# A small load of 64 KiB issued ahead of the first 8 MiB load of a row normalisation

## The chip, the cores and the metric

The kernel runs on one core of a Trainium2 chip. The metric is device time in microseconds (us), the median of several executions; lower is better.

## The reference

```python
x: 1024 x 4096 float32, eps = 1e-12
norm = sqrt(sum(x ** 2, axis=-1, keepdims=True) + eps)
out = (x / norm).astype(float32)
```

16 MiB are read and 16 MiB are written, with little arithmetic for each byte.

## The kernel before

The 1024 rows are cut into two tiles. Each of the 128 partitions of a tile holds four whole rows, which lie side by side in memory, so a load of a tile consists of 128 contiguous pieces of 64 KiB. Both tiles fit into SBUF, so both loads are issued at once:

```python
R = 4
n_tiles = N // (P * R)                                   # 2
x_t = x.rearrange("(p t r) d -> t p (r d)", t=n_tiles, r=R)
...
for i in range(n_tiles):
    g = RowGroups(nc, io, stats, scratch, D, R, eps_t)
    load = nc.sync.dma_start(out=g.flat(), in_=x_t[i])   # 128 pieces of 64 KiB
    to_front(nc, load.ins)
    groups.append(g)
```

`to_front` moves a load to the very front of SyncE's program, ahead of the barrier at which the engines of the core meet. For each tile VectorE squares and sums one row and ScalarE three; a square root and a reciprocal follow, and the rows are scaled in place. The last row of the first tile is scaled by both engines (ScalarE 7/8 of it). Then the tile is stored by one DMA:

```python
for i, g in enumerate(groups):
    g.square_dve(R - 1)
    g.square_act(0)
    g.norm(0)
    g.scale(0)
    ...                                                  # rows 1, 3 and 2 alike
    if i < n_tiles - 1:
        g.scale_by_both(2)                               # cut = 7 * D // 8
    else:
        g.scale(2)
    store = nc.sync.dma_start(out=out_t[i], in_=g.flat())
```

## Time and profile before

| | kernel before |
|---|---|
| time, median of 6 | 81.88 us (81.67 to 81.95) |
| span of the profiled execution | 79.9 us |
| share of the span in which the 16 DMA engines moved packets | 97.6% |
| VectorE, ScalarE busy | 33%, 37% |
| 32 rows of 16 packets of 64 KiB at 2.42 us | 77.4 us |

I call 16 packets, one on each DMA engine, a row (of packets; the rows of the matrix are another thing); the kernel has 32 of them, 8 for each load and each store. The compute engines mostly wait, and what they wait for is data. Here are the page's busy line, its memory line, and the two longest waits (engine and line, what it waited for, us in total, times, longest):

```profile
DVE 26.7 (33%) x21; ACT 29.7 (37%) x23; POOL 0.2 (0%) x4
HBM read 16.78 MB, written 16.78 MB: 420 GB/s over the span
```

```profile
DVE sq_dve L42 <- DMA xt<-in_x_dram: 25.7, 2, 20.4
ACT sq_act L33 <- DMA xt<-in_x_dram: 21.7, 2, 19.3
```

### The profile page before, as it was taken

The numbers are of one execution on the slowest core, as the hardware profiler recorded it, in microseconds if no ns is written. First come the engines' busy times: TensorE is split into PE (matmuls) and PEld (weight loads), VectorE is DVE, ScalarE is ACT, GpSimd is POOL, SyncE is SP. The second block draws the span as 40 slices with busy tenths as digits, with TensorE's granted clock in tenths as the row PEclk, the third lists the DMA queues.
The fourth block names the chain that finished last, engine by engine and source line by source line (L and its number), as shares of the span: only waits on it lengthen the run. The fifth ranks groups of instructions, "written<-read, shape, count | busy, mean of one in ns | idle before, by whom it ended". The sixth has DMA issues, their size and how long they took to land.

```text
span 79.9 us, 93 instructions
## 1 busy us (share of the span) xinstructions
DVE 26.7 (33%) x21; ACT 29.7 (37%) x23; POOL 0.2 (0%) x4
## 2 busy tenths in 40 slices
DVE  0000000000099599960049995999200000000000
ACT  3200000000099999989349999950000000000000
POOL 1000000000000000000000000000000000000000
DMA  9099996599996699993899991999974999965990
GB/s 492 33 525 525 525 525 295 230 525 525 525 525 262 262 525 525 525 525 164 361 525 525 525 459 66 525 525 525 525 328 197 525 525 525 525 295 230 525 525 0
DMA packets 576, 33.55 MB, mean 420 GB/s; under 512 B 64, under 2 KB 64, under 8 KB 64
## 3 DMA queue, kind: packets, MB, share of 16 engines
q1 hardware_dynamic: 576, 33.55, 97.6%
HBM read 16.78 MB, written 16.78 MB: 420 GB/s over the span
## 4 chain that ended last, share of the span: by engine, by line
DMA 51%; ACT 10%; DVE 9%; SPq 0%; issue 0%
DMA xt<-in_x_dram 51%; ACT sq_act L33 9%; DVE xt L64 9%; ACT rstd L53 1%; SPq L219 0%; DVE rstd L59 0%
## 5 line engine op out<-in xcount | busy, mean ns | idle before, releaser
L33 ACT ACTIVATE sq_act<-xt 128x4096 f32<-128x4096 f32 x6 | 21.7, 3609 | 21.7 <-DMA xt<-in_x_dram 21.7
L42 DVE SCALAR_TENSOR_TENSOR sq_dve<-xt 128x4096 f32<-128x4096 f32 x2 | 8.8, 4424 | 25.7 <-DMA xt<-in_x_dram 25.7
L64 DVE TENSOR_SCALAR xt<-xt,rstd 128x4096 f32<-128x4096 f32 x7 | 16.5, 2353 | 0.2
L72 ACT ACTIVATE xt<-xt,rstd 128x3584 f32<-128x3584 f32 x1 | 3.3, 3282 | 0.2 <-DVE rstd L59 0.2
L53 ACT ACTIVATE rstd<-ssq,eps_t 128x1 f32<-128x1 f32 x8 | 2.1, 289 | 0.1
L59 DVE RECIPROCAL rstd<-rstd 128x1 f32<-128x1 f32 x8 | 1.3, 159 | 2.4 <-ACT rstd L53 2.4
L33 ACT ACT_TABLE_LOAD x1 | 1.3, 1283 | 1.3 <-PEq L257 1.3
L53 ACT ACT_TABLE_LOAD x1 | 1.3, 1283 | 0.0
L33 ACT ACTIVATION_READ_ACCUMULATOR sq_act<-xt 128x1 f32 x6 | 1.1, 186 | 0.0
L211 DVE MEMSET eps_t<- 128x1 f32 x1 | 0.1, 59 | 1.3 <-PEq L257 1.3
L78 DVE TENSOR_SCALAR xt<-xt,rstd 128x512 f32<-128x512 f32 x1 | 0.5, 486 | 0.0
L42 DVE DVE_READ_ACCUMULATOR sq_dve<-xt 128x1 f32 x2 | 0.2, 82 | 0.0
L257 POOL MEMSET const-bfloat16-1.0<- 128x1 bf16 x1 | 0.1, 103 | 0.0
L257 POOL MEMSET const-uint8-127<- 128x1 uint8 x1 | 0.1, 102 | 0.0
L257 POOL MEMSET const-float32-0.0<- 128x1 f32 x1 | 0.1, 100 | 0.2 <-issue 0.2
L257 POOL MEMSET const-float32-1.0<- 128x1 f32 x1 | 0.1, 99 | 0.0
## 6 DMA issues: line engine op xcount, KB each, us to landing
xt<-in_x_dram SPq DMA_DIRECT2D x2, 31.2
out_dram<-xt SPq DMA_DIRECT2D x2, 22.5
```

The costliest lines, as they stand in the source:

```text
L33: self.nc.scalar.activation(out=sq_a, in_=self.x[:, r], func=ACT_F.Square, accum_out=self.ssq[:, r : r + 1],)
L42: self.nc.vector.scalar_tensor_tensor(out=sq_v, in0=self.x[:, r], scalar=1.0, in1=self.x[:, r], op0=ALU.mult, op1=ALU.mult, accum_out=self ...
L53: self.nc.scalar.activation(out=self.rstd[:, r : r + n], in_=self.ssq[:, r : r + n], func=ACT_F.Sqrt, bias=self.eps_t,)
L59: self.nc.vector.reciprocal(out=self.rstd[:, r : r + n], in_=self.rstd[:, r : r + n])
L64: self.nc.vector.tensor_scalar_mul(out=self.x[:, r], in0=self.x[:, r], scalar1=self.rstd[:, r : r + 1])
L72: self.nc.scalar.activation(out=self.x[:, r, :cut], in_=self.x[:, r, :cut], func=ACT_F.Copy, scale=rstd,)
L78: self.nc.vector.tensor_scalar_mul(out=self.x[:, r, cut:], in0=self.x[:, r, cut:], scalar1=rstd)
L211: nc.vector.memset(eps_t, eps)
L257: nc = _bacc.Bacc("TRN2", target_bir_lowering=False, num_devices=1)
```

## The change

The first 512 bytes of each of the 128 pieces of the first tile are loaded once more, into a tile that nobody reads, ahead of everything else. The intent: let a small load meet the slow start, so that the big one runs at full rate from its first byte.

```diff
+    heads = scratch_pool.tile([P, D // 32], F32)
+    to_front(nc, nc.sync.dma_start(out=heads, in_=x_t[0][:, : D // 32]).ins)
 
     groups = []
     for i in range(n_tiles):
```

## The prediction

> **What bounds the kernel now.** I read the page's queue part first, then the chain that ended last in order of time, then the two load issues, then short windows at the two ends of the span.
>
> The DMA queue (packets, MB, share of the span that 16 DMA engines were occupied) and the chain (start us, us, what):
>
> ```profile
> q1 hardware_dynamic: 576, 33.55, 97.6%
> ```
>
> ```profile
> 0.00 0.38 SPq L219
> 0.38 0.05 issue
> 0.43 40.69 DMA xt<-in_x_dram
> ```
>
> The queue has 16 engines occupied for 97.6% of 79.9 us, which is 78.0 us of the span. VectorE has 26.7 us and ScalarE 29.7 us of work, a third each. The chain continues from the second load through the arithmetic of the second tile and breaks off at the last scale, before the last store; but the stream of data is not interrupted while that arithmetic runs, because the first store is already queued at 38.71 us:
>
> ```profile
> 38.71 18.13 SPq L239 DMA_DIRECT2D out_dram<-xt  x2
> ```
>
> The two stores are issued at 38.71 and about 56.5 us (38.71 + 18.13 less one issue of 0.35). The first is issued before the second load has landed (41.1 us), the second before the first store is through (the 16 engines finish it at about 60 us). So compute is hidden, and the time is head + stream + tail of the DMA engines.
>
> Short windows show the head and the tail. The columns are the window, its length, the busy time of three engines, the clock, the DMA share and GB/s. From the values I infer that a packet is counted whole in the window in which it starts (a share of 4.34 can't be otherwise), so a window of 0.5 us gives both a count (GB/s times 0.5 us over 65,536 bytes) and a mean duration (share times 0.5 us times 16, over the count):
>
> ```profile
> 0.50:1.00 0.50, 0.00 (x0) 0.00 (x0) 0.00 (x0) 1.00 0.00 0
> 1.00:1.50 0.50, 0.06 (x1) 0.23 (x1) 0.00 (x0) 1.00 4.34 1442
> 1.50:2.00 0.50, 0.00 (x0) 0.50 (x1) 0.00 (x0) 1.00 1.29 524
> 2.00:2.50 0.50, 0.00 (x0) 0.50 (x1) 0.00 (x0) 1.00 0.30 131
> ...
> 4.00:4.50 0.50, 0.00 (x0) 0.00 (x0) 0.00 (x0) 1.00 4.23 1835
> 4.50:5.00 0.50, 0.00 (x0) 0.00 (x0) 0.00 (x0) 1.00 0.60 262
> ...
> 76.50:77.00 0.50, 0.00 (x0) 0.00 (x0) 0.00 (x0) 1.00 4.84 2097
> ```
>
> What to see: nothing starts before 1.00 us. Then 11 packets start by 1.50 (1442 x 0.5 / 65.5 = 11), 4 by 2.00 and one after 2.00: one for each of 16 engines, spread over more than half a microsecond. The 11 early ones last 4.34 x 0.5 x 16 / 11 = 3.16 us each, the 4 next 2.58, the last 2.4. The second row (14 + 2 packets from 4.00 on) lasts 4.23 x 8 / 14 = 2.42 us each, and so does the last row, whose 16 packets all start between 76.50 and 77.00. 32 rows of 2.42 are 77.4 us, the floor of this kernel. What is above it in the span: 1.0 us before the first packet, (4.34 + 1.29 + 0.30) x 8 / 16 = 2.97 us for the mean first packet against 2.42, so 0.55 us lost in the first row, some 0.4 us of spread between engines, and about half a microsecond after the last packet. The 1.9 us between span and measured time (79.9 against 81.77 in the profiled run) lie outside the program's instructions.
>
> A detail decides much below: early starters are slow, late starters are not. An engine that starts after 2.00 runs at full speed at once. So the first row's loss does not look like a fixed fee that each engine pays for its first packet; it looks like a phase, ending some 1.7 to 2.1 us after the first issue, before which no engine runs at full rate.
>
> **What the Trainium skill says.** "DMA: Bandwidth & Descriptors", section "Latency and other measured facts", gives about 600 ns to the first byte of a DMA issued from SyncE. The trace agrees: the first issue ends at 0.38 us and the first packets start just after 1.00, 0.62 later. The same page, "Where 436 GB/s comes from", puts the ceiling of the 16 engines at 435 GB/s; 16 x 65,536 bytes in 2.42 us are 433 GB/s, so the stream is at that ceiling and no change at its front can speed it up. The same page, "Queues, rings and completion order", says that each engine consumes descriptors in ring order: the head pieces come before the first big pieces on every engine. And its "Rules for kernel authors" warn that transfers under 64 KB are mostly overhead; the new load is 128 x 512 bytes, exactly 64 KiB. No run here shows yet what that costs on this path. I found no page that speaks of a slow first transfer or of warming one up.
>
> **The change, part by part.** It adds one load of 64 KiB in 128 pieces into a tile that nobody reads, and moves it to the very front, before the first big load. It removes nothing. The intent must be that the small load meets the slow phase, so that the big one runs at full speed from its first byte.
>
> Issue: a load's issue holds the SyncE queue for 0.38 to 0.43 us:
>
> ```profile
> L219 SPq DMA_DIRECT2D xt<-in_x_dram x2: 383/404/426, 0.0 to 0.4; - x2
> ```
>
> So the first big load is issued at about 0.43 us in place of 0.00, and its first packets can start at 1.00 + 0.43 = 1.43 at the earliest. Data: 4 KiB for each engine; at the measured 65,536 bytes in 2.42 us that is 0.15 us, an estimate without any fee per piece. It falls between 1.0 and 1.43, in which the engines would have nothing else, so on the path it costs little or nothing. The end: one more completion to be waited for, 16 small packets that land 78 us before the end; nothing. Compute: ScalarE and VectorE leave the start barrier about 0.4 us later (its table load starts at 1.26 and is over at 2.54), while the first data land at 21.8; nothing. Space: 512 bytes of a partition; nothing.
>
> What remains is the time at which each engine's first big packet ends. Now the mean first packet ends at about 1.3 + 2.97 = 4.27 (1.3 is my estimate of the mean start from the counts: 11 near 1.1, 4 near 1.7, one near 2.05), the slowest between 4.50 and 5.00 (two packets of the second row start there). If the phase is fully absorbed and the starts bunch at 1.43, the end is 1.43 + 2.42 = 3.85: at best 0.65 to 0.7 us saved from the slowest engine. If nothing is absorbed, everything moves by the issue: +0.43. These two bracket the likely effect.
>
> **Rivals.**
>
> 1. The head load absorbs the slow phase (the author's intent). For: 11 of 16 first packets take 3.16 us instead of 2.42, and something must be cold. It would give -0.2 to -0.7 us: 81.15 to 81.65. Against: the late starters pay nothing.
>
> 2. The phase belongs to the start of the whole DMA system and ends at a fixed time after the first access, whatever is read. Then the big packets start at 1.43 but still crawl until 1.7 to 2.1: no change, or plus the 0.15 us of data: 81.85 to 82.0. For: early starters slow, late ones not, all reaching full rate at about the same moment.
>
> 3. The phase belongs to each load's own pieces being prepared and handed to the engines, 128 pieces at a time (the starts are spread over a microsecond, 1.00 to past 2.00). The head load has as many pieces as the big one, so it can't be cheaper to prepare; the big load's pieces come after, so +0.43 us, and up to +1.0 if the two preparations don't overlap at all: 82.3 to 82.85. For: the spread of the starts. Against: pieces of the second load and of both stores are prepared while others move, so the trace gives no second example.
>
> 4. The small pieces are slow in themselves (the page's warning), some 0.1 us a piece and 8 on each engine: +0.4 on top of the second rival. No duration for it in this trace.
>
> None of them touches the 77.4 us of stream, so none reaches 2% (1.64 us). Most of the first row's loss and of the start's 1.0 us would have to vanish together to be faster by that much, and the issue of the big load is even later than before.
>
> **Range and chances.** I give the first rival 0.4 (it is a deliberate, odd-looking change, of the kind one keeps after it has helped; centre 81.45), the second 0.3 (centre 81.9), the third and fourth together 0.3 (centre 82.3). The weighted mean is 0.4 x 81.45 + 0.3 x 81.9 + 0.3 x 82.3 = 81.84; the middle of the distribution is a little lower, and I say 81.8. The range from 81.2 to 82.4 leaves out only the full gain of the first and the bad half of the third. Faster by over 2% (below 80.2) and slower by over 2% (above 83.5) get 0.02 each.
>
> **What the profile after would show.** Three issues at the front, the third ending at about 1.25 us. 128 more packets of 512 bytes in the queue's count, plus 16 small ones. If the first rival holds, the windows from 1.4 to 2.0 us hold all 16 big starts, and share over count gives 2.42 us for them. If the second, big packets start near 1.43 and still last 2.8 to 3.1. If the third, their starts move by the issue or more, with the same spread. The last row's starts, 76.50 to 77.00 now, tell the whole effect: they must move by what the total time moves. I would be wrong altogether if that row stays and the time still changes (an effect after the end of the stream), or if the packets of the middle rows no longer last 2.42 us.

## The result, and the profile after

The changed kernel takes 82.47 us (82.33 to 82.75, 6 runs) against 81.88: 0.59 us more. The ratio is 1.0081, with a 95% interval from 1.0061 to 1.0100. Ratios here are the mean time of one kernel's runs over the mean of the other's in the same rounds, so they aren't quite the ratio of the medians. It is the same within 2%, but clearly slower, and 0.07 us above the predicted range.

The chain of the changed kernel, in order of time (start us, us, what), and the line of the DMA issues for the small load (KB, us from issue to landing):

```profile
0.00 0.38 SPq L219
0.38 0.05 issue
0.43 0.42 SPq L224
0.86 0.04 issue
0.90 40.94 DMA xt<-in_x_dram
```

```profile
heads<-in_x_dram SPq DMA_DIRECT2D x1, 64.0 KB, 2.0
```

L219 is now the small load and L224 the first of the big ones: it is issued at 0.43 us, where the kernel before had it at 0.00. The small load lands 2.0 us after its issue, which means after the big load's packets have started.

The same short windows as in the prediction, of the changed kernel:

```profile
0.50:1.00 0.50, 0.00 (x0) 0.00 (x0) 0.00 (x0) 1.00 0.00 0
1.00:1.50 0.50, 0.00 (x0) 0.00 (x0) 0.00 (x0) 1.00 0.43 127
1.50:2.00 0.50, 0.06 (x1) 0.26 (x1) 0.00 (x0) 1.00 5.70 1839
2.00:2.50 0.50, 0.00 (x0) 0.50 (x1) 0.00 (x0) 1.00 0.65 262
...
4.50:5.00 0.50, 0.00 (x0) 0.00 (x0) 0.00 (x0) 1.00 4.28 1835
5.00:5.50 0.50, 0.00 (x0) 0.00 (x0) 0.00 (x0) 1.00 0.60 262
...
77.00:77.50 0.50, 0.00 (x0) 0.00 (x0) 0.00 (x0) 1.00 3.93 1704
77.50:78.00 0.50, 0.00 (x0) 0.00 (x0) 0.00 (x0) 1.00 0.91 393
```

The window from 1.00 to 1.50 holds only small packets (127 GB/s for 0.5 us are 64 KB). From 1.50 to 2.00 start 14 big ones (1839 x 0.5 / 65.5), which last 5.70 x 8 / 14 = 3.26 us, and two more follow after 2.00 with 2.6. So the first row is as slow as before, indeed a little slower. The second row is back near the normal, at 4.28 x 8 / 14 = 2.45, and the last row, which began entirely between 76.50 and 77.00, now begins between 77.00 and 78.00. The second load's first row starts 0.61 us late (table below) and the last row 0.63, so nearly the whole loss arises at the front.

To follow that over many runs I use a few numbers, taken as means over the 16 packets of a row from the packet records of the trace. "Full rate after issue" is the mean end of the first big row, less one normal duration of 2.42 us, less the time at which that load was issued: the time from issue to the moment from which the engine might as well have run at full rate.

| kernel | first big load issued | its first packets last | full rate after issue | second load's first row starts |
|---|---|---|---|---|
| before | 0.00 | 2.97 | 1.86 | 21.19 |
| after | 0.43 | 3.16 | 2.03 | 21.81 (+0.61) |
| e1, small load second | 0.00 | 3.14 | 1.83 | 21.35 (+0.16) |
| e2, 16 pieces in front | 0.45 | 3.03 | 1.90 | 21.67 (+0.48) |
| e4, second load late | 0.00 | 3.11 | 1.87 | 21.22 (+0.03) |
| e6, small load from ScalarE | 0.00 | 3.16 | 1.85 | 21.36 (+0.17) |
| e9, big load after landing | 3.10 | 3.20 | 1.87 | 24.30 (+3.11) |
| e10, pieces of 2 KiB in front | 0.43 | 2.75 | 2.00 | 21.76 (+0.57) |

These are single profiled executions. In the four rows of the table in which a big load goes first at 0.00, and in e18 below (1.89), the full rate comes after 1.83 to 1.89 us; so much do single traces scatter.

### The profile page after: what moved, and what is told of

It is laid out like the page before. It is cut to its first block, busy times and chain, and to the rows that moved or that the text cites. A ratio compares the mean times of both kernels' runs of the same rounds, so it can differ in the third digit from the quotient of the medians.

```text
span 80.6 us, 95 instructions
## 1 busy us (share of the span) xinstructions
DVE 26.7 (33%) x21; ACT 29.7 (37%) x23; POOL 0.2 (0%) x4
## 4 chain that ended last, share of the span: by engine, by line
DMA 51%; ACT 10%; DVE 9%; SPq 1%; issue 0%
DMA xt<-in_x_dram 51%; ACT sq_act L33 9%; DVE xt L64 9%; ACT rstd L53 1%; SPq L224 1%; SPq L219 0%; DVE rstd L59 0%
```

## The experiments

**Theory A**: the loss is the big load's issue, put back by 0.43 us by the one in front of it, plus a smaller term for the small load's own pieces; the slow first row is not absorbed, because it belongs to each load that starts on engines with nothing to move. **Rivals**: B, the small load costs its 0.6 us as work wherever it stands; C, the slow first row is something cold that a small load could take away if it had the chance; D, the slow row is made by the next load being prepared beside it; E, it comes of 16 engines that walk in step through addresses a power of two apart.

The diffs are shortened: unchanged or repeated branches are left out. Those of e1, e2, e5, e6, e9 and e10 are against the changed kernel, those of e3, e4, e7, e11 and e18 against the kernel before, and the others against the run that the text names.

### e1_heads_second: the small load behind the first big one

```diff
-    to_front(nc, nc.sync.dma_start(out=heads, in_=x_t[0][:, : D // 32]).ins)
...
         to_front(nc, load.ins)
         groups.append(g)
+        if i == 0:
+            to_front(nc, nc.sync.dma_start(out=heads, in_=x_t[0][:, : D // 32]).ins)
```

> The same 64 KiB load of 128 pieces, but queued behind the first big load and ahead of the second. Theory A (the cost is the delay of the first big load's issue, 0.43 us, and what it does to that load's first pieces): the front is as in the kernel before, first big packets at 1.0 us, and only the data of the small load remain, 4 KiB an engine or about 0.2 us (8 x 25 ns, the duration of its packets in the changed kernel): 81.9 to 82.1. Theory B (the small load costs its 0.6 us as work, wherever it stands): 82.4 to 82.5.

Measured: 82.16 us (81.97 to 82.25) against 81.86, ratio 1.0034 (1.0022 to 1.0047), so 0.30 more; the front is as before (table). The small load's packets move behind the first big load, from 21.0 to 21.5 us, and the row of the second load is 0.16 late. (The trace is of the fastest of the five executions, 81.97; its last row is 0.19 late.) Half of the loss has gone with nothing but the order of two issues. B falls; the time is a little over A's 82.1.

### e2_heads_16: 16 of the 128 pieces, in front

```diff
-    to_front(nc, nc.sync.dma_start(out=heads, in_=x_t[0][:, : D // 32]).ins)
+    to_front(nc, nc.sync.dma_start(out=heads[:16], in_=x_t[0][:16, : D // 32]).ins)
```

> The small load stays in front, with 16 of its 128 pieces (one for each engine, 8 KiB in all). If only the issue counts (0.43 us for any number of pieces): 82.3, 0.15 less than the changed kernel because the slow first row is then as before. If the pieces themselves or their preparation count: nearer to before, under 82.1. If the 128 pieces cost nothing at all: 82.45 as in the changed kernel.

Measured: 82.26 us (82.20 to 82.36) against 81.86, ratio 1.0048 (1.0034 to 1.0062), so 0.40 more. One eighth of the pieces leaves two thirds of the loss, which is what an issue costs:

```profile
0.00 0.39 SPq L219 DMA_DIRECT2D heads<-in_x_dram  x1
...
0.45 0.89 SPq L224 DMA_DIRECT2D xt<-in_x_dram  x2
```

The issue of 16 pieces takes as long (0.39 us) as that of 128 (0.38), and the big load is issued at 0.45.

### e6_heads_from_act: the small load from ScalarE's queue

```diff
-    to_front(nc, nc.sync.dma_start(out=heads, in_=x_t[0][:, : D // 32]).ins)
+    to_front(
+        nc,
+        nc.scalar.dma_start(out=heads, in_=x_t[0][:, : D // 32]).ins,
+        mybir.EngineType.Activation,      # the engine whose program it leads
+    )
```

> The small load of 128 pieces is issued by ScalarE at the front, beside the first big load from SyncE, so that no issue stands ahead of the big one. Theory A (issue 0.4 plus pieces 0.2): only the pieces are left, 82.05 to 82.2, big first packets from 1.0 us. If the small load helps once its issue costs nothing: under 81.8. If two queues at the front disturb each other: 82.4 and over.

Measured: 82.17 us (82.16 to 82.29) against 81.85, ratio 1.0043 (1.0030 to 1.0055), 0.32 more. The two queues, the small load's time to landing, and the window of the first packets:

```profile
q1 hardware_dynamic: 576, 33.55, 97.5%
q10 hardware_dynamic: 144, 0.07, 0.3%
...
heads<-in_x_dram ACTq DMA_DIRECT2D x1, 64.0 KB, 22.1
```

```profile
1.00:1.50 0.50, 0.06 (x1) 0.25 (x1) 0.00 (x0) 1.00 5.18 1704
```

The big load's first packets are back at 1.0 us and last 5.18 x 8 / 13 = 3.19 us (1704 x 0.5 / 65.5 = 13). But the run does not show whether a small load helps that costs no issue, for it didn't go first: its first packet starts at 3.90 us, its eight packets on an engine move one after each of the first eight big ones, and it lands only 22.1 us after its issue. The run shows the cost of the pieces, 0.17 us in the second load's row. That the time fits A's figure is partly luck: 0.15 us is a gap between the loads' mean end (40.68) and the stores' mean start (40.83).

### e4_load1_late: the second load not prepared beside the first

```diff
+        if i == 1:
+            nc.vector.memset(g.x[:, 0], 0.0)
         load = nc.sync.dma_start(out=g.flat(), in_=x_t[i])
-        to_front(nc, load.ins)
+        if i == 0:
+            to_front(nc, load.ins)
```

> No small load; the second big load is issued only after a fill of part of its tile by VectorE, at about 4 us or later, in place of 0.43 us. If the preparation of the next load's pieces is what slows the first row (and in the changed kernel two loads are prepared beside it, so more), the first packets last 2.42 in place of 2.97 us and the time falls by up to 0.55: 81.3 to 81.5. If the slow row has nothing to do with the load behind: 81.85 to 81.95, first packets 2.9 to 3.0 us.

Measured: 81.90 us (81.81 to 82.02) against 81.86, ratio 1.0005 (0.9992 to 1.0017). The second load was issued at 5.2 us, and in the window in which 14 of the first packets start they last 5.52 x 8 / 14 = 3.15 us:

```profile
1.00:1.50 0.50, 0.00 (x0) 0.50 (x1) 0.00 (x0) 1.00 5.52 1835
```

D falls.

### e3_rows: the first load in four loads of 16 KiB pieces

```diff
-        load = nc.sync.dma_start(out=g.flat(), in_=x_t[i])
+        for r in range(R):                                 # first tile only
+            load = nc.sync.dma_start(out=g.x[:, r], in_=x_t[i][:, r * D : (r + 1) * D])
+            to_front(nc, load.ins)
```

> No small load; the first load is cut into four loads of 128 pieces of 16 KiB, issued one behind the other. Normal duration of such a piece is 2.42 / 4 = 0.60 us. This is a magnifying glass for the slow first row: a phase in time gives slow 16 KiB packets only until about 2.0 us (one to two rows, 0.55 us lost in all, 81.9 us); a loss spread evenly over each engine's first 64 KiB gives four rows of 0.74 us. If the slow row comes of big pieces being handed out, it goes away, and the time falls to about 81.4.

Measured: 83.02 us (82.96 to 83.22) against 81.86, ratio 1.0146 (1.0132 to 1.0160). That is above all three expected times, and two things have to be kept apart. In the front, the first 16 packets of 16 KiB last 1.26 us in the mean, where 0.61 is normal, and the next 16 last 0.62: the whole loss lies in each engine's first 16 KiB, as a phase in time would have it. The second load's first row starts at 21.26 (before: 21.19), so the front is neither better nor worse. The 1.16 us are lost in the middle. Windows of e3_rows in which the last row of the second load starts:

```profile
37.50:38.00 0.50, 0.00 (x0) 0.00 (x0) 0.00 (x0) 1.00 0.44 131
38.00:38.50 0.50, 0.00 (x0) 0.00 (x0) 0.00 (x0) 1.00 6.33 1966
```

15 packets start after 38.00 and last 6.33 x 8 / 15 = 3.38 us in place of 2.42. What differs there is the first store: with data arriving row by row the first tile is done early, and its store is issued at 29.35 us instead of 38.71.

### e8_rows_store_late: the same, with that store held back

```diff
+        if i < n_tiles - 1:                                # ahead of g.norm(R - 1)
+            for width in (D, D, 3 * D // 4):
+                nc.vector.memset(sq_dve[:, :width], 0.0)
+            last = g.ssq[:, R - 1 : R]                     # last + 0: the value stays
+            nc.vector.scalar_tensor_tensor(out=last, in0=last, scalar=1.0,
+                in1=sq_dve[:, :1], op0=ALU.mult, op1=ALU.add)
```

> As e3_rows (four loads of 16 KiB pieces), but the first store is held by fills on VectorE until about 38.9 us, where the kernel before has it (38.7), in place of 29.35. In e3_rows the front was as before, and the last 16 packets of the second load took 3.0 to 3.8 us in place of 2.42 with the store queued behind them. If a store that is queued long before the loads end causes that: those packets last 2.42 again and the time is 81.9 to 82.1. If it comes of the smaller pieces: 82.9 to 83.1 as in e3_rows.

Measured: 83.77 us (83.73 to 84.02) against 81.85. The time is a miss: the fills took longer than I had reckoned (VectorE paused 0.7 to 0.9 us between them), the store was issued at 41.65, and nothing moved between the end of the loads (40.8) and 42.5. But the row in question is decided:

```profile
38.00:38.50 0.50, 0.47 (x2) 0.00 (x0) 0.00 (x0) 1.00 4.84 2097
```

All 16 packets start here and last 4.84 x 8 / 16 = 2.42. So not the piece size but the early store behind them had made them slow. e18 shows the same without any small pieces.

### e7_pitch80: pieces 80 KiB apart instead of 128

```diff
-    x_t = x.rearrange("(p t r) d -> t p (r d)", t=n_tiles, r=R)
+    rows = [5, 3]; cut = P * rows[0]                       # out_t alike
+    x_t = [x[:cut].rearrange("(p r) d -> p (r d)", r=rows[0]),
+           x[cut:].rearrange("(p r) d -> p (r d)", r=rows[1])]
```

> No small load; the two tiles have 5 and 3 rows for each partition in place of 4 and 4, taken as contiguous blocks, so that the 128 pieces of the first load start 80 KiB apart (not a power of two) in place of 128 KiB, and its packets are 40 KiB (1.51 us at the rate of the rest). If the slow first row comes of 16 engines that run in step through addresses a power of two apart: first packets of about 1.5 us, and up to 0.5 us gained, 81.4. If it is the fill of an empty queue: first packets 1.51 + 0.55 to 0.75 = 2.05 to 2.25, time about 81.9 plus what 128 more pieces cost (under 0.2), if the stores still follow without a gap.

Measured: 89.37 us (89.19 to 89.63) against 81.85. The time is a miss and says nothing about the front: five rows of the first tile weren't computed in time, its store was issued at 47.08 and the engines idled after the loads had ended at 41.3. The front is clear, though. All 16 first packets, of 40 KiB, start in one window:

```profile
1.00:1.50 0.50, 0.06 (x1) 0.15 (x1) 0.00 (x0) 1.00 4.74 1311
```

They last 4.74 x 8 / 16 = 2.37 us where 1.51 is normal, a loss of 0.86; that is more than either expectation had (1.5, or 2.05 to 2.25). E falls for this pitch.

### e5_heads_landed_first: the big load only after the small one has landed (failed)

```diff
+        if i == 0:
+            nc.vector.memset(g.x[:, 0, :512], 0.0)
-        load = nc.sync.dma_start(out=g.flat(), in_=x_t[i])
-        to_front(nc, load.ins)
+        nc.sync.dma_start(out=g.flat(), in_=x_t[i])
```

> The small load in front, and the first big load issued only when the small one has landed (2.0 us in the changed kernel), held by a short fill of part of its tile: slower on purpose. It gives the idea of the change every chance. If something is cold once and a small load takes it away: the first big packets last 2.42 us and the mean engine is at full rate about 1.3 us after the big load's issue. If the slow first packets belong to every load that starts on an empty queue: they last 2.9 to 3.2 us again and the mean engine is at full rate 1.83 to 1.87 us after that issue, as in the kernel before and three runs of the first call. Time: before plus the lateness of the issue, 2.4 to 2.8 us, that is 84.2 to 84.7; with a gain from the small load half a microsecond less.

Measured: 105.70 us (105.64 to 105.89) against 81.85. The second load doesn't depend on the fill, and in the compiled order it slipped ahead of the first: it was issued at 0.79 us, before the small load had landed, and the first tile came only at 42 us. The run doesn't test what it was to test. Its front is of use all the same. The small packets were over at 1.47 us, the first big one started at 1.75, and the big load's first packets still lasted 3.07 us; full rate came 1.82 us after its issue.

### e9_heads_landed_both_held: the repeat

```diff
+        nc.vector.memset(g.x[:, 0, :2048], 0.0)            # for both tiles
         load = nc.sync.dma_start(out=g.flat(), in_=x_t[i])
-        to_front(nc, load.ins)
```

> The repeat of e5_heads_landed_first, in which the second load had slipped ahead of the first: now both big loads are held by fills, so that the first big load is issued only at about 3 to 3.7 us, a microsecond or more after the small one has landed. Slower on purpose. Cold once and taken away by the small load: first big packets 2.42 us, full rate 1.3 us after the big load's issue, time before + issue - 0.55. Belongs to every load that starts on an empty queue: first packets 2.9 to 3.2 us, full rate 1.83 to 1.87 us after the issue, time before + issue, about 85.0 to 85.6.

Measured: 85.31 us (85.29 to 85.74) against 81.85, 3.46 more. The timeline and the windows:

```profile
0.00 0.37 SPq L219 DMA_DIRECT2D heads<-in_x_dram  x1
...
3.10 0.33 SPq L226 DMA_DIRECT2D xt<-in_x_dram  x1
```

```profile
4.00:4.50 0.50, 0.50 (x1) 0.00 (x0) 0.00 (x0) 1.00 6.03 1966
```

The small load landed 1.7 us after its issue; the big one was issued 1.4 us after that. Its first 15 packets last 6.03 x 8 / 15 = 3.22 us all the same, and it reaches full rate 1.87 us after its issue, which is the number of the other loads of 64 KiB pieces that start on idle engines (1.82 to 1.89 in before, e1, e4, e5, e6, e18 and here). C falls, as far as a small load goes that is over when the big one begins. Of the 3.46 us, 3.11 are the later load; the rest is about the size of a gap of 0.38 us between the loads' mean end (43.66) and the stores' mean start (44.04).

### e10_heads_2k: four times the bytes, in front

```diff
-    heads = scratch_pool.tile([P, D // 32], F32)
-    to_front(nc, nc.sync.dma_start(out=heads, in_=x_t[0][:, : D // 32]).ins)
+    heads = scratch_pool.tile([P, D // 8], F32)
+    to_front(nc, nc.sync.dma_start(out=heads, in_=x_t[0][:, : D // 8]).ins)
```

> The small load in front with pieces of 2 KiB in place of 512 bytes (256 KiB in all, 16 KiB or 0.61 us an engine at full rate). In e3_rows the first 16 KiB of each engine took the whole loss of the first row and the next 16 KiB none. If the small load was only too short to hide the issue of the big one (0.43) and the wait for first data: the big first packets now last about 2.42, and the cost is the larger of issue and data, about 0.6 to 0.7: 82.4 to 82.6, no more than with a quarter of the bytes. If issue and data add up: 0.43 + 0.6 or more, 82.9 to 83.1.

Measured: 82.44 us (82.42 to 82.70) against 81.85, ratio 1.0081 (1.0068 to 1.0095). That is the changed kernel's ratio to the last digit, with 192 KiB more to move. The expected 2.42 us of the big first packets is not reached, but they fall to 2.75. So a head with more data does begin to take the wait on itself, and its bytes are then hidden in that wait; issue and bytes don't simply add up.

### e11_head_in_tile: a head of 4 KiB, without duplicate bytes

```diff
-        load = nc.sync.dma_start(out=g.flat(), in_=x_t[i])
+        cut = D // 4                                       # first tile only
+        head = nc.sync.dma_start(out=g.flat()[:, :cut], in_=x_t[i][:, :cut])
+        to_front(nc, head.ins)
+        load = nc.sync.dma_start(out=g.flat()[:, cut:], in_=x_t[i][:, cut:])
```

> The idea without its duplicate bytes: the first 4 KiB of each piece go to their real place by a first load (32 KiB an engine, 1.2 us), the other 60 KiB of the piece by a second load behind it. The issue of the second is hidden behind the data of the first. If smaller first pieces start the stream sooner: under 81.7. If the start of the stream is the same whatever goes first: 81.85 to 82.0[...].

Measured: 82.12 us (82.03 to 82.51) against 81.85, ratio 1.0042 (1.0025 to 1.0060), above both expectations. For the big load absorption is complete: the first packets of the big load (60 KiB) last 2.27 us, exactly 60/64 of 2.42. The wait is now in the head, whose first packets of 4 KiB last 0.2 to 0.67 us instead of 0.16. The loads even ended 0.22 us earlier in the mean (40.30 against 40.52). It was lost again at the store, for a reason that has nothing to do with DMA:

```profile
21.76 1.28 ACT L33 ACT_TABLE_LOAD   x1 [21.76 <-DMA xt<-in_x_dram]
26.78 1.28 ACT L53 ACT_TABLE_LOAD   x1
39.95 0.35 SPq L245 DMA_DIRECT2D out_dram<-xt  x1
```

ScalarE's first table load stood at 1.26 us in the kernel before; now it waits for data. The store is issued 1.24 us later than before, and the engines idle 0.55 us between the loads' mean end and the stores' mean start (40.85).

### e12_head_4k_table_early, e13_head_8k_table_early, e14_head_512_table_early

The same with the table load brought back, and with heads of 4 KiB, 8 KiB and 512 bytes (`cut = D // 4`, `D // 2`, `D // 32`):

```diff
     nc.vector.memset(eps_t, eps)
+    early = scratch_pool.tile([P, 1], F32)
+    nc.scalar.activation(out=early, in_=eps_t, func=ACT_F.Square)
```

> e11_head_in_tile with one more thing put right: there ScalarE's table load had slipped from 1.3 us to 21.8 us (it waited with the first square for the data), so the first store was issued at 39.95 in place of 38.71, and between the mean end of the loads (40.30) and the mean start of the stores (40.85) the engines idled 0.55 us. A square of one column at the start brings the table load back. The loads of e11 were 0.22 us earlier than in the kernel before (40.30 against 40.52). If that gain is real and the idle gap was all that ate it: 81.6 to 81.7, first store issued before 39 us. If the front gains nothing: 81.85 to 81.95.

> The same with a head of 8 KiB of each piece (64 KiB an engine). If smaller first pieces start the stream sooner (16 KiB pieces in e3_rows: nothing; 4 KiB in e11: 0.22 to 0.25): between the two, 81.65 to 81.85. If it is the length of the head that counts and not the size of its pieces: as e12 or lower, 81.6.

> The changed kernel without its duplicate bytes: the head of 512 bytes goes to its place in the tile, the rest of each piece follows. It splits the 0.6 us of the change: no data are added, so if the extra 0.2 us over the issue (82.26 with 16 pieces, 82.47 with 128) are the data of the small load, this costs the issue alone, 82.2 to 82.3. If they are the 128 pieces themselves or the wait of the big load behind them, 82.4 to 82.5. If 0.5 KiB heads start the stream sooner as 4 KiB heads seem to: under 82.1.

Measured, against 81.90: e12 82.02 us (82.00 to 82.06), ratio 1.0015 (1.0000 to 1.0030); e13 81.91 (81.82 to 82.19), 1.0006 (0.9988 to 1.0023); e14 82.59 (82.51 to 82.61), 1.0082 (1.0067 to 1.0097). In e12 and e13 the loads ended at 40.29 and 40.27, again some 0.23 us early, but the stores began at 40.49 and 40.46: the order of the square roots had changed, the store was issued at 39.26 and 39.15, and a gap of 0.2 us opened.

e14 is the change without its added bytes. Its time is no better, but it too has that gap of 0.21 us. Its second load starts at 21.52, 0.33 after the kernel before and 0.29 earlier than in the changed kernel. That is what can be expected of the issue (0.43), less 0.15 for bytes that the big load no longer moves (eight packets of 2.40 us in place of 2.42), plus 0.05 in the first row. So the front costs the issue here and hardly more; the time doesn't show it.

### e15_head_4k_ordered, e16_head_8k_ordered (failed)

```diff
+        if i == 0:                     # rows 0 and 3 in one square root and reciprocal
+            pair = slice(0, R, R - 1)
+            nc.scalar.activation(out=g.rstd[:, pair], in_=g.ssq[:, pair],
+                                 func=ACT_F.Sqrt, bias=eps_t)
+            nc.vector.reciprocal(out=g.rstd[:, pair], in_=g.rstd[:, pair])
```

> e12_head_4k_table_early with the square roots of rows 0 and 3 of the first tile in one instruction, because in e12 the order of ScalarE's work had changed as well, so that the first store was issued at 39.26 (38.71 in the kernel before) and each engine idled 0.21 us between the mean end of its loads (40.29) and the mean start of its stores (40.49). If that late store alone hides the 0.23 us by which the loads are earlier: store issued by about 38.8, no gap, 81.6 to 81.75. If the gap comes back for another reason: 81.9 to 82.0 again, and the 0.23 us is not to be had.

> The same for the 8 KiB head of e13 (loads' mean end 40.27, stores' mean start 40.46, store issued at 39.15): 81.6 to 81.75 if the late store was all, about 81.9 if not.

Measured: 83.73 us (83.51 to 83.93) and 83.72 (83.63 to 83.82) against 81.86. The compiled order changed again: VectorE ran two scalings ahead of the last reciprocal, and in e15 the store was issued at 41.52. What is of use: with the same loads in front, their mean end was 40.51 and 40.48 this time, against 40.29 and 40.27 in e12 and e13, and 40.52 in the kernel before. The gain in the front is not steady.

### e17_head_8k_cut58 and its control e18_before_cut58

```diff
-        cut = 7 * self.D // 8
+        cut = 5 * self.D // 8          # e17: in e13; e18: in the kernel before
```

> e13_head_8k_table_early with the last scaling of the first tile shared otherwise (ScalarE 5/8, VectorE 3/8 in place of 7/8 and 1/8), so that it ends and the first store is issued about 0.9 us earlier, at some 38.3 us, with nothing else moved. It is the same aim as e15 and e16, which missed: there the reordering put the store at 41.5 us. If the late store was all that ate the gain: 81.6 to 81.75. If the gain of the front is not steady (the loads' mean end was 40.27 to 40.30 in e11, e12, e13 and 40.48 to 40.51 in e15 and e16, with the same loads at the front): 81.75 to 81.9.

> Control: the kernel before with only that other sharing, store at about 37.8 instead of 38.7. No effect expected (81.8 to 81.9), unless an earlier store slows the last row of loads, as it did where the store stood at 29.35 (e3_rows): then 82 and over, and e17 has to be read against this run.

Measured: e17 81.86 us (81.71 to 81.95) against 81.93, ratio 0.9991 (0.9978 to 1.0003); e18 82.41 (82.28 to 82.46), ratio 1.0057 (1.0043 to 1.0071). e17 has its store at 38.48, no gap, loads that end at 40.33, and still no time that can be told from the kernel before. It is the best that came out of the idea, and it doesn't beat the kernel before.

The control went the way that its expectation named second, and is the more instructive. Store issue and the windows of the last row of loads, in e18:

```profile
37.86 0.35 SPq L239 DMA_DIRECT2D out_dram<-xt  x1
```

```profile
37.50:38.00 0.50, 0.00 (x0) 0.33 (x1) 0.00 (x0) 1.00 0.77 262
38.00:38.50 0.50, 0.00 (x0) 0.00 (x0) 0.00 (x0) 1.00 5.16 1835
```

14 packets from 38.00 on last 5.16 x 8 / 14 = 2.95 us in place of 2.42. A store issued 0.85 us earlier than in the kernel before made it 0.5 us slower.

## Why the prediction was wrong

**What bounds the kernel** held. The middle rows and the last row still last 2.42 us, and the last row moved by 0.63 us in the mean (76.74 to 77.37) where the time moved by 0.59 (0.69 between the two executions that were profiled). Next to nothing happened after the stream.

**Issue** held. The big load is issued at 0.43 us, as worked out, and the third issue ends at 1.33 (1.25 had been expected). e2 shows that term nearly alone: 0.40 us.

**Data** is the first step that failed: "It falls between 1.0 and 1.43, in which the engines would have nothing else, so on the path it costs little or nothing." I had their size about right: 8 on each engine of 25 to 27 ns, 0.2 us. But they don't all fit in front: they run from 1.00 to 1.61 us, ten of the 128 start after 1.43, and the first big packet starts at 1.50. The second load starts 0.61 late, which is 0.18 more than the issue, and 0.17 of that is there when the first row ends (full rate 2.03 in place of 1.86). e2 with 16 pieces takes 82.26 and the changed kernel 82.47; e1 and e6, with the pieces and without an issue in front, lose 0.30 and 0.32 in time and 0.16 to 0.17 in that row. So this term, which I set at nothing, is about 0.2 us: 0.16 to 0.18 in the traces, while the times of e1 and e6 have a little more in them (see there). What of it is bytes and what is the big load's wait behind 128 pieces is not settled. In e5 and e9, where the small packets were over before the first big one started, there is no such term (1.82 and 1.87). That fits a cost that arises only where the small packets run into the big load's start. But in e14 they do so too (they end at 1.56, the first big one starts at 1.51), and full rate comes after 1.90 us; the 0.29 by which its second load starts earlier than in the changed kernel is half (0.15) bytes that aren't moved twice. e10 has four times the bytes and costs no more; that speaks against a simple sum.

**The choice of weights** is the second, and it decided the miss: it put the centre 0.1 us under the kernel before, where 0.59 over it was measured. I gave the first rival, absorption, 0.4 and a centre of 81.45 with the words "it is a deliberate, odd-looking change, of the kind one keeps after it has helped". That isn't a reading of the profile. The profile spoke against it, and I had written so: "the late starters pay nothing". In the changed kernel no absorption is found: the first packets last 3.16 us. Even in e9, with 1.4 us between landing and the next issue, they last 3.20. Without that share the mean of the second and of the third and fourth rivals is (81.9 + 82.3) / 2 = 82.1, and a range as wide as mine around it would have held 82.47.

**The second rival**, a phase that ends at a fixed time after the first access, fell too. Full rate comes 1.82 to 1.89 us after the issue of the load in question, whether that is at 0.00, 0.79 or 3.10 us. So the slow phase that I had read from the windows is there, but it goes with the load and not with the start of the program. **The third** was right in its first half: everything moves by the issue, with nearly the same spread of starts (0.9 us; 1.0 before). Its bad half (preparations that don't overlap, up to +1.0) didn't occur. **The fourth**, 0.1 us a piece, was four times too high; a piece takes 25 to 27 ns.

Why a small head can't do what it is meant to do is shown by e3, e10 and e11 together. Where a stream of loads starts on idle engines, each engine's first data take longer than normal: by 0.55 to 0.78 us with 64 KiB pieces (before and e9), by 0.65 on 16 KiB in e3, by 0.86 on 40 KiB in e7. The load that goes first pays. A head of 4 KiB an engine, as in the change, is over in 0.2 us, before the wait is, so the big load pays in full. With 16 KiB the two share it (2.75 us for the big packets), and with 32 KiB the head pays all of it (2.27 us for 60 KiB). Then the big load looks perfect in the profile, but most of the wait is only paid under another name: the heads of e11 to e13 and e15 to e17 took 0.33 to 0.51 us longer, over an engine's eight pieces, than eight pieces at their later pace (0.16 us for 4 KiB, 0.31 for 8). The loads ended 0.19 to 0.25 us early in four of these six runs, and in none was the kernel shown to be faster.

What the engines wait for in that time, no run here shows. Idleness alone it is not, for stores don't pay it. In e5 the engines had moved nothing for 22 us when the first store began:

```profile
41.50:64.00 22.50, 19.03 (x16) 21.91 (x18) 0.00 (x0) 1.00 0.00 0
64.00:64.50 0.50, 0.50 (x1) 0.50 (x1) 0.00 (x0) 1.00 4.60 1966
```

The 15 packets that start here last 4.60 x 8 / 15 = 2.45 us, and the store reaches full rate 0.94 us after its issue, half of what a load takes. It is the same in e8, e9 and e15, whose first store also starts on idle engines.

## What to carry to other kernels

In a kernel that a stream of transfers bounds, a transfer put in front of the first big one costs about its full issue time, unless it carries data of its own to cover it (e11 to e13). A warm-up gains only if it ends a wait and doesn't merely pay it in the big transfer's place. So ask for the time from issue to full rate, and whether it belongs to the start of the program or to each load that starts on idle engines. A change being odd and deliberate is no evidence of its gain; give chances only from what the profile says. And when a front is moved by a fraction of a microsecond, look at the next seam as well: three runs won 0.2 us at the loads and lost it again because a store came 0.4 to 1.2 us later.

## What the Trainium skill lacked or had wrong

- "DMA: Bandwidth & Descriptors", "Latency and other measured facts": its 600 ns to the first byte agrees (0.62 us from the end of the issue to the first packet). Missing is the time to full rate, which is what counts for a stream: for a load on idle engines 1.82 to 1.89 us from the start of the issue in seven runs with 64 KiB pieces, with first packets of 2.97 to 3.20 us instead of 2.42; for a store on idle engines 0.94 us in four runs (e5, e8, e9, e15).
- The same page, "Issuing engines are not separate DMA queues", says that issuing from several engines saves only the sequencer's issue time. e6 agrees in that 82.17 from ScalarE stands against 82.47 from SyncE and both queues' packets share the engines. But the order changed as well: issued 0.13 us after the big load, the small one's packets came behind the first big ones (from 3.90 us on), and it landed after 22.1 us.
- The same page, "Rules for kernel authors", says transfers under 64 KB are mostly overhead. For this 64 KiB load in 128 pieces the overhead is the issue, 0.38 us for 128 pieces and 0.39 for 16; a piece of 512 bytes takes 25 to 27 ns of an engine.
- No page that I found tells when to issue a store behind a stream of loads. Issued before the last row of loads begins (37.9 to 38.3 us), it makes that row slow: 3.38 us when issued at 29.35, 2.96 at 37.86. Issued at 38.71 it leaves it at 2.43, and the stores follow without a gap. Where the store was issued only 0.35 to 1.12 us before the loads' mean end (e11 to e14), a gap of 0.2 to 0.55 us opened, and at 1.67 us (e6) one of 0.15; in the kernels before and after it is issued 1.81 and 1.72 us before that end, with at most 0.02. Why the early store slows the loads, no run shows.
